# The last matrix product of a two-block layer stack as seven products of half blocks, on one core

## The chip, the cores and the metric

The kernel runs on one core of a Trainium2 chip. The metric is device microseconds of one launch: 3528.63 us, the median of 3 runs (3527.05 to 3533.05). One more execution was taken with the hardware profiler; all rows below come from it.

## The reference, cut to what matters

Two transformer-like blocks run one after the other on 512 tokens of width 2048. The change concerns the last lines of the second block, its feed-forward part and the final norm:

```python
        x = x + y @ w_out[l]
        h = rms_norm(x, norm2_g[l])
        x = x + (jax.nn.silu(h @ ffn_w_gate[l]) * (h @ ffn_w_up[l])) @ ffn_w_down[l]
    return rms_norm(x, final_norm_g)
```

Here `ffn_w_gate` and `ffn_w_up` are 2048 x 5632, `ffn_w_down` is 5632 x 2048, all in float32.

## The kernel before

Every float32 operand is split into two float32r tiles, a high part (`wh` for weights) and a rest (`wl`): `split` (L136, L122) casts on ScalarE (ACT) and subtracts on VectorE (DVE). A product of two operands is then three TensorE matmuls: high x high, low x high and high x low.

`finish` (L1710) runs three stages. The first is the output projection `w_out`, which leaves the residual `x3d` in DRAM. The second, the **gate and up stage**, goes through the hidden width in 11 chunks `c` of 512 columns. It computes both products with seven half-size products for eight (a scheme of Strassen's kind): `fast_group` (L1639) takes weight blocks a11, a12 (gate, upper and lower half of the rows) and a21, a22 (up), builds sums of them on VectorE (`chained`, L1650 on), and works through products 1, 7, 5, 6, 4, 3, 2. A product has four **halves** here (index `u`): one weight tile of 128 x 2 x 512, its split, and 12 matmuls of 512 columns, 8 with `wh` and then 4 with `wl`. Weight tiles come through a pool `fr` of 10 buffers. The split tiles have three buffers in turn (two of `wp2`, one of `fw`), so a split can be written once TensorE is through with the half three places before. The chunk's activation is transposed (`pt`) and stored to `ud` in DRAM.

The third, the **down stage**, is the plain product `ud @ ffn_w_down`: for each of 10 chunks (`down`) and each of 4 column strips, 4 rows of weights times 4 token tiles times 3 matmuls into four `psm` banks, each added to the accumulator `facc` on VectorE. `facc` is loaded from `x3d` first, with `fg`, by 1 MB transfers. The eleventh chunk stands alone as the **last block**: its eight weight tiles are split beforehand, and each token tile is normed and stored right after its matmuls.

Transfers are issued from SP's queue in program order. A scheduler places instructions in each engine's queue by priority and its own estimate; on the chip each queue runs strictly in the order in which it was written.

Of the kernel before, what the change touches and what calls it, by code (L numbers as in the profile page):

```python
# [93 lines left out]
class Kernel:  # L94
# [1508 lines left out]
    def fast_operands(self, pool, za, zb, tiles):  # L1603
        ta, tb = slice(0, 256), slice(256, 512)
        x5 = self.t(pool, [128, 4, 256], F32, "fx5")
        x6 = self.t(pool, [128, 4, 256], F32, "fx6")
        x7 = self.t(pool, [128, 4, 256], F32, "fx7")
# [4 lines left out]
        for i, x in ((1, za[:, :, ta]), (7, x7), (5, x5), (6, x6), (4, None), (3, zb[:, :, tb]), (2, zb[:, :, ta])):  # L1612
            if i == 4:
                x = x7
# [8 lines left out]
    def halves(self, raw, pools):  # L1623
        pools.append(pools.pop(0))
        h = self.t(pools[0], [128, 2, 512], F32R, "wh")
        l = self.t(pools[0], [128, 2, 512], F32R, "wl")
        self.split(h, l, raw)
        return h, l

    def fast_group(self, srcs, X, rp, cp, wps, parts):
# [22 lines left out]
        def part(i, u, opens):  # L1655
            with tc.high_priority(self.ahead):
                h, l = self.halves(weight[i](u), wps)
            at = [(2 * u + kk, kk, t) for kk in range(2) for t in range(2)]

            for j, kk, t in at:  # L1660
                xh, xl = (x[:, j % 4, t * 128:t * 128 + 128] for x in X[j // 4][i])
                self.mm(ps[i][:, t, :], xh, h[:, kk, :], opens and j == 0, False, not opens)
                self.mm(ps[i][:, t, :], xl, h[:, kk, :], False, False, not opens)
            for j, kk, t in at:
                xh = X[j // 4][i][0][:, j % 4, t * 128:t * 128 + 128]
                self.mm(ps[i][:, t, :], xh, l[:, kk, :], False, j == 7, not opens)
# [43 lines left out]
    def finish(self):  # L1710
        tc, nc, a = self.tc, self.nc, self.a
        NC = 11
        ud = self.t(self.dr, [4 * NC, 128, NX], F32, "ud")
        x3d = self.t(self.dr, [4, 128, D], F32, "x3d")
        wg, wu, wd = a["ffn_w_gate_2"][0], a["ffn_w_up_2"][0], a["ffn_w_down_2"][0]
        with self.pool("ff0", 1) as f0:
# [3 lines left out]
            with self.pool("opx", 2) as opx:  # L1720
                X = []
                made = [0]

# [4 lines left out]
                with self.pool("w21", 1) as p1, self.pool("w22", 2) as p2, self.pool("w23", 3) as p3:  # L1728
# [3 lines left out]
                    for n, b in enumerate((0, 2, 1, 3)):  # L1732
# [22 lines left out]
                        else:  # L1755
                            X.append(self.fast_operands(p1, za, z, tiles))
# [10 lines left out]
                with self.pool("fr", 10, side="right") as rp, self.pool("fc", 1) as cp, self.pool("fu", 2) as up, self.pool("fw", 1) as fw:  # L1767
                    wps = [self.wp2, self.wp2, fw]
                    for c in range(NC):
                        cs = slice(c * 512, c * 512 + 512)  # L1770
                        parts = ((0, 1), (2, 3)) if c == 0 else ((0, 1, 2, 3),)
                        for half, (g, u) in zip((1, 0), self.fast_group((wg[:, cs], wu[:, cs]), X, rp, cp, wps, parts)):
                            pt = [self.t(pt_, [128, 512], F32, "pt") for _ in range(2)]
                            for t in range(2):
# [5 lines left out]
                                for f in range(4):  # L1780
                                    o = f % 2 * 256 + t * 128
                                    self.tr(pt[f // 2][:, o:o + 128], s[:, f * 128:f * 128 + 128])
                            for k in range(2):
# [4 lines left out]
            self.raw_pool = self.pool("wq", 3, side="right")  # L1788
            self.wp = self.raw_pool.__enter__()
            self.psum_pools(4, 4)  # L1790
            with self.pool("ff1", 2) as p1, self.pool("ff2", 1) as p2:
                acc = self.t(p2, [128, 4, D], F32, "facc")
                for t in range(4):
                    nc.sync.dma_start(out=acc[:, t, :], in_=x3d[t])
                fg = self.t(p2, [128, D], F32, "fg")
                nc.sync.dma_start(out=fg, in_=a["final_norm_g_2"].rearrange("(o d) -> o d", o=1).to_broadcast([128, D]))

                def hidden(c):
                    u = self.four(F32)
                    nc.sync.dma_start(out=u, in_=ud[c * 4:c * 4 + 4].rearrange("f p t -> p f t"))  # L1800
                    h4, l4 = self.four(F32R), self.four(F32R)
                    self.split(h4, l4, u)
                    return [(h4[:, j, :], l4[:, j, :]) for j in range(4)]

                def down(c, hs):
# [8 lines left out]
                hs = [hidden(0), hidden(1)]  # L1814
                for c in range(NC - 1):
                    down(c, hs[c])
                    if c + 2 < NC:
                        hs.append(hidden(c + 2))

                c = NC - 1  # L1820
                W = []
                for b in range(4):
                    h4, l4 = self.four(F32R), self.four(F32R)
                    for k in range(0, 4, 2):
                        raw = self.t(self.wp, [128, 2, 512], F32, "raw")
# [57 lines left out]
```

## Time and profile before

| | us |
|---|---|
| median of 3 runs | 3528.63 |
| the profiled execution, its time | 3531.79 |
| its span, first to last instruction | 3530.0 |
| gate and up stage, first `un` to the stage change | 2202.5 to about 3026 |
| down stage without the last block | 3025.8 to 3475.7 |
| last block, to the end | 3475.7 to 3530.0 |

The span is what the trace covers; 1.8 us of the execution lie outside it. The profiled execution is 3.2 us above the median of the runs. Matmuls are pipelined: a row's duration is longer than the distance to the next one, so a stretch is costed by the distance.

### The profile page before, as it was taken

The page shows a single profiled execution, that of the slowest core. Times are in us where ns is not written, and L with a number is a line of the kernel's source. Part 1 is how long each engine was busy: PE and PEld are TensorE (multiplying, and loading weights), DVE is VectorE, ACT ScalarE, POOL GpSimd, SP SyncE. Part 2 cuts the span into 40 slices and gives each one's busy share as a digit, 9 for nine tenths or more (in the row PEclk, how much of TensorE's full clock was granted, in tenths as well). Part 3 has the DMA queues.
Part 4 walks back from the last instruction along what each step waited for, and adds up shares of the span by engine and source line. Part 5 has one row for each costly group of instructions (what it writes and reads, how often), then busy time and mean ns, then how long its engine had stood idle before and what let it go on. Part 6 is the DMA issues. An engine that isn't in the chain of part 4 may idle for free.

```text
span 3530.0 us, 48454 instructions
## 1 busy us (share of the span) xinstructions
PE 3438.7 (97%) x18738; PEld 2740.7 (78%) x18738; DVE 2213.8 (63%) x3495; ACT 1367.9 (39%) x2223; POOL 55.1 (2%) x50
## 2 busy tenths in 40 slices
PE   6999999999999999999999998999999999999998
PEld 3488888777778787788777786888888888788887
DVE  4367875466555455764566557778887788555545
ACT  3234444465433323433233334444444444322122
POOL 0000000000000000000000000000000000000000
PEclk8999999999999999999999999999999999999999
DMA  8833433222343443434434543444334335533333
GB/s 283 276 90 89 113 115 109 70 80 63 88 149 124 138 131 97 116 108 132 132 105 144 163 137 108 131 128 123 114 108 125 120 114 160 185 119 119 102 96 108
DMA packets 352602, 442.21 MB, mean 125 GB/s; under 512 B 45871, under 2 KB 200179, under 8 KB 351731
## 3 DMA queue, kind: packets, MB, share of 16 engines
q1 hardware_dynamic: 349456, 437.82, 40.8%
q8 instruction: 147, 2.41, 0.3%
q10 hardware_dynamic: 2915, 1.29, 0.1%
q14 instruction: 84, 0.69, 0.1%
HBM read 383.45 MB, written 55.57 MB: 124 GB/s over the span
## 4 chain that ended last, share of the span: by engine, by line
PE 90%; DMA 5%; DVE 3%; issue 1%; ACT 1%; SPq 0%; POOL 0%; DVEq 0%; POOLq 0%; ACTq 0%
PE acc L112 41%; PE psm L112 23%; PE pp L112 23%; DMA wm<-in_w_mod_dram 2%; PE psm L116 2%; DVE wl L122 1%; PE pt L116 1%; DMA xr<-in_x_dram 0%; DMA raw<-in_ffn_w_down_dram 0%; DVE ga L132 0%; DMA ym<-ysd 0%; DMA fr<-in_ffn_w_gate_dram 0%; DVE op L122 0%; DMA xr<-in_ctx_dram 0%; DMA fr<-in_ffn_w_up_dram 0%
## 5 line engine op out<-in xcount | busy, mean ns | idle before, releaser
L112 PE MATMUL acc<-op,wh 128*128 128x512 f32 (+2 forms) x4160 | 1245.0, 389 | 12.2 <-ACT op L136 4.1
L112 PEld LDWEIGHTS acc<-op,wh 128*128 128x128 f32 (+1 forms) x4160 | 765.1, 190 | 198.8 <-issue 32.2
L122 DVE TENSOR_TENSOR wl<-raw,wh 128x512 fp32r<-128x512 f32 (+4 forms) x464 | 420.8, 907 | 631.6 <-ACT wh L136 597.9
L112 PE MATMUL acc<-op,wl 128*128 128x512 f32 (+2 forms) x2080 | 768.3, 389 | 4.9 <-DVE wl L122 4.7
L136 ACT CAST wh<-raw 128x512 fp32r<-128x512 f32 (+4 forms) x464 | 369.1, 796 | 991.4 <-PE acc L112 597.5
L112 PE MATMUL pp<-wh,op 128*128 128x512 f32 x2112 | 529.7, 393 | 10.1 <-ACT wh L136 10.1
L136 ACT CAST wh<-fr 128x1024 fp32r<-128x1024 f32 x308 | 322.9, 1052 | 400.8 <-PE pp L112 352.8
L112 PEld LDWEIGHTS pp<-wh,op 128*128 128x128 f32 x2112 | 397.5, 188 | 98.8 <-ACT wh L136 10.2
L112 PEld LDWEIGHTS acc<-op,wl 128*128 128x128 f32 (+1 forms) x2080 | 389.7, 189 | 98.9 <-issue 18.5
L122 DVE TENSOR_TENSOR wl<-fr,wh 128x1024 fp32r<-128x1024 f32 x308 | 371.0, 1219 | 103.8 <-ACT wh L136 67.0
L112 PE MATMUL psm<-wh,op 128*128 128x512 f32 x1280 | 396.6, 391 | 7.3 <-DVE facc L122 7.3
L112 PEld LDWEIGHTS psm<-wh,op 128*128 128x128 f32 x1280 | 241.6, 189 | 58.2 <-issue 7.7
L112 PE MATMUL pp<-wl,op 128*128 128x512 f32 x1056 | 285.4, 392 | 0.1
L112 PE MATMUL psm<-wl,op 128*128 128x512 f32 x640 | 250.2, 391 | 0.3 <-DVE wl L122 0.3
L122 DVE TENSOR_TENSOR fr<-fr,fr 128x1024 f32<-128x1024 f32 x176 | 210.9, 1220 | 47.4 <-DMA fr<-in_ffn_w_gate_dram 28.8
L112 PEld LDWEIGHTS pp<-wl,op 128*128 128x128 f32 x1056 | 197.7, 188 | 43.8 <-DVE wl L122 0.8
L122 DVE TENSOR_TENSOR facc<-facc,psm 128x512 f32<-128x512 f32 x176 | 117.9, 685 | 60.1 <-PE psm L112 54.3
L112 PEld LDWEIGHTS psm<-wl,op 128*128 128x128 f32 x640 | 120.8, 189 | 25.6 <-DVE wl L122 0.7
L112 PE MATMUL acc<-wh,op 128*128 128x256 f32 x576 | 113.6, 292 | 0.0
L112 PEld LDWEIGHTS acc<-wh,op 128*128 128x128 f32 x576 | 90.9, 191 | 5.0 <-issue 3.6
L112 PE MATMUL pp<-wh,opx 128*128 128x512 f32 x352 | 93.8, 399 | 0.0
L112 PE MATMUL acc<-wl,op 128*128 128x256 f32 x288 | 84.4, 294 | 1.0 <-DVE wl L122 0.9
(474 smaller groups left out, 3521.3 us busy)
## 6 DMA issues: line engine op xcount, KB each, us to landing
raw<-in_w_in_dram SPq DMA_DIRECT2D x216, 256.0 KB, 2.8
fr<-in_ffn_w_gate_dram SPq DMA_DIRECT2D x88, 512.0 KB, 4.2
fr<-in_ffn_w_up_dram SPq DMA_DIRECT2D x88, 512.0 KB, 4.2
raw<-in_ffn_w_down_dram SPq DMA_DIRECT2D x88, 512.0 KB, 4.0
wm<-in_w_mod_dram SPq DMA_DIRECT2D x64, 512.0 KB, 5.5
raw<-in_w_out_dram SPq DMA_DIRECT2D x64, 512.0 KB, 3.8
raw<-in_w_in_dram SPq DMA_DIRECT2D x240, 128.0 KB, 2.3
wm<-in_w_mod_dram SPq DMA_DIRECT2D x64, 256.0 KB, 2.9
```

The lines of the kernel that those rows point to most:

```text
L112: self.nc.tensor.matmul(out, lhsT=l, rhs=r, start=start, stop=stop, skip_group_check=more)
L116: self.nc.tensor.transpose(out, x, self.ident[0:n, 0:n])
L122: (e or self.nc.vector).tensor_tensor(out=out, in0=x, in1=y, op=op)
L136: self.nc.scalar.copy(h, x)
```

## The change

The down stage now uses seven products for eight as well, over pairs of chunks. `X` is the hidden state of two chunks, cut by tokens (first and last 256) and by rows of the hidden width; the weights of two chunks are cut into a11, a12, a21, a22 for each 1024 columns (`v` = 0, 1).

- The token operands 5, 6, 7 and 4 are sums of the transposed activation. They are made in the gate and up stage by four VectorE instructions in each of 10 chunks, and seven tiles instead of four go to `ud`.
- In the down stage, each pair of chunks loads seven operand tiles and splits them. For each `v` the products run in the order 1, 7, 2, 5, 4, 6, 3, with two halves each. Only product 5's weight sum (a21 + a22) is made on VectorE (`both`). The sums for 7, 6 and 3 are made in place in a11's tile by accumulating transfers that GpSimd's queue (POOL) issues (`plus`): a11 + a21, then + a22, then + a12. Product 7 follows product 1, and 3 follows 6, on the same tile.
- PSUM stays with the gate and up stage's three `pp` double banks; products 2, 4 and 3 are accumulated on top of 1, 7 and 5. `facc` is first written by products, and `x3d` is added to it by eight accumulating transfers.
- The pool `fr` of 10 buffers is kept through the down stage, and the last block's weights and `fg` are loaded through it early.

Core of the diff:

```diff
-                                v = self.t(up, [128, 2, 256], F32, "v")
-                                nc.scalar.copy(v, pt[k].rearrange("p (f t) -> p f t", f=2))
-                                f = c * 4 + k * 2
-                                nc.sync.dma_start(out=ud[f:f + 2, :, half * 256:half * 256 + 256].rearrange("f p t -> p f t"), in_=v)
+                                nc.scalar.copy(vs[k], pt[k].rearrange("p (f t) -> p f t", f=2))
+                            if half:
+                                b12, b22 = vs
+                                continue
+                            b11, b21 = vs
+                            out = [(1, b11), (2, b21), (3, b22)]
+                            if c < NC - 1:
+                                x5, x6 = (self.t(up, [128, 512], F32, "s").rearrange("p (f t) -> p f t", f=2) for _ in range(2))
+                                self.tt(x5, b11, b12, ALU.subtract)
+                                self.tt(b12, b12, b22, ALU.subtract)
+                                self.stt(x6, b22, -1.0, x5, ALU.mult, ALU.subtract)
+                                out += [(5, x5), (7, b12), (6, x6)]
...
+                            for i, x in out:
+                                nc.sync.dma_start(out=ud[i - 1, c].rearrange("f p t -> p f t"), in_=x)
+                            if c < NC - 1:
+                                self.tt(b21, b21, x6, ALU.add)
+                                nc.sync.dma_start(out=ud[3, c].rearrange("f p t -> p f t"), in_=b21)
...
-                for t in range(4):
-                    nc.sync.dma_start(out=acc[:, t, :], in_=x3d[t])
...
-                    for b in range(4):
-                        ps = [self.psm() for _ in range(4)]
-                        self.block(wd[c * 512:c * 512 + 512], [(b * 512, 512)], 4,
-                                   [(ps[t], "t", (t, 0), hs, True, True) for t in range(4)])
-                        for t in range(4):
-                            v = acc[:, t, b * 512:b * 512 + 512]
-                            self.tt(v, v, ps[t], ALU.add)
...
+                order = (1, 7, 2, 5, 4, 6, 3)
+
+                def operands(c):
+                    X = {}
+                    with tc.high_priority(400):
+                        for i in order:
+                            x = raw().rearrange("p a (b t) -> p (a b) t", t=256)
+                            nc.sync.dma_start(out=x, in_=ud[i - 1, 2 * c:2 * c + 2].rearrange("g f p t -> p (g f) t"))
+                            o = self.four(F32R)
+                            h, l = (o[:, k:k + 2, :].rearrange("p a (b t) -> p (a b) t", t=256) for k in (0, 2))
+                            self.split(h, l, x)
+                            X[i] = (h, l)
+                    return [X]
...
+                    def plus(name, u):
+                        nc.gpsimd.dma_start(out=W["a11", u], in_=load(name, u), accum_op=ALU.add)
+                        return W["a11", u]
+
+                    def both(u):
+                        x, y = plain("a21", u), plain("a22", u)
+                        self.tt(x, x, y, ALU.add)
+                        return x
+
+                    weight = {
+                        1: lambda u: plain("a11", u), 7: lambda u: plus("a21", u), 2: lambda u: plain("a12", u),
+                        5: both, 4: lambda u: W["a22", u], 6: lambda u: plus("a22", u), 3: lambda u: plus("a12", u),
+                    }
...
+                    onto = {2: 1, 4: 7, 3: 5}
+                    to = {1: U, 7: A22, 2: A11, 5: A22, 4: A21, 6: U, 3: A12}
+                    for i in order:
+                        ps[i] = ps[onto[i]] if i in onto else bank()
+                        for u in range(2):
+                            with tc.high_priority(self.ahead):
+                                h, l = self.halves(weight[i](u), wps)
+                            self.product(X, i, ps[i], h, l, 2 * u, i not in onto, 3)
+                        if c == 0 and i not in (5, 6):
+                            nc.scalar.copy(to[i], ps[i])
+                        else:
+                            self.tt(to[i], to[i], ps[i], ALU.subtract if i == 5 else ALU.add)
+                    if c == 0:
+                        for t in range(4):
+                            o = slice(v * 1024, v * 1024 + 1024)
+                            nc.gpsimd.dma_start(out=acc[:, t, o], in_=x3d[t][:, o], accum_op=ALU.add)
```

`product` holds the 12 matmuls that `part` in `fast_group` had, in the same order; `order` gives the seven products their numbers.

How the instructions stand. First TensorE's queue at the change of stage. Before, the transposes (`pt`) of the last activation stand among the down stage's first matmuls (`psm`):

```order
L112 MATMUL psm_4435_25726<-wh_4442_25761,op_4430_25716 128x512
L112 MATMUL psm_4436_25727<-wh_4442_25761,op_4429_25715 128x512
L116 MATMUL pt_4420_25660<-ident_11_107,s_4422_25662 128x128 x2
L116 MATMUL pt_4421_25661<-ident_11_107,s_4422_25662 128x128 x2
L116 MATMUL pt_4420_25660<-ident_11_107,s_4423_25670 128x128 x2
L116 MATMUL pt_4421_25661<-ident_11_107,s_4423_25670 128x128 x2
L112 MATMUL psm_4436_25727<-wl_4443_25762,op_4429_25715 128x512
L112 MATMUL psm_4436_25727<-wh_4442_25761,op_4430_25716 128x512
L112 MATMUL psm_4437_25728<-wh_4442_25761,op_4429_25715 128x512
L112 MATMUL psm_4437_25728<-wl_4443_25762,op_4429_25715 128x512
L112 MATMUL psm_4437_25728<-wh_4442_25761,op_4430_25716 128x512
```

Now, behind product 1's first half (`pp_4463` with `wh_4465`) and the transposes of `s_4427`, comes product 7 (`pp_4470`), then the next transposes, and only then product 1's second half (`wh_4468`):

```order
L116 MATMUL pt_4425_25663<-ident_11_107,s_4428_25673 128x128 x2
L116 MATMUL pt_4426_25664<-ident_11_107,s_4428_25673 128x128 x2
L112 MATMUL pp_4470_25864<-wh_4471_25866,op_4452_25798 128x512 x8
L112 MATMUL pp_4470_25864<-wl_4472_25867,op_4452_25798 128x512 x4
L116 MATMUL pt_4440_25751<-ident_11_107,s_4442_25753 128x128 x2
L116 MATMUL pt_4441_25752<-ident_11_107,s_4442_25753 128x128 x2
L116 MATMUL pt_4440_25751<-ident_11_107,s_4443_25761 128x128 x2
L116 MATMUL pt_4441_25752<-ident_11_107,s_4443_25761 128x128 x2
L112 MATMUL pp_4463_25826<-wh_4468_25847,op_4450_25793 128x512 x8
L112 MATMUL pp_4463_25826<-wl_4469_25848,op_4450_25793 128x512 x4
L112 MATMUL pp_4470_25864<-wh_4473_25883,op_4452_25798 128x512 x8
L112 MATMUL pp_4470_25864<-wl_4474_25884,op_4452_25798 128x512 x4
```

The two halves of products 1 and 7 have moved into each other, with the transposes between them. In the nine later pairs of `c` and `v` the products stand one after the other.

Second VectorE in the middle of the down stage. Before, two splits (`wl`) and four additions to `facc` alternate:

```order
L122 TENSOR_TENSOR wl_4592_26732<-raw_4590_26729,wh_4591_26731 128x1024
L122 TENSOR_TENSOR wl_4599_26770<-raw_4597_26767,wh_4598_26769 128x1024
L122 TENSOR_TENSOR facc_4426_25706<-facc_4426_25706,psm_4583_26695 128x512
L122 TENSOR_TENSOR facc_4426_25706<-facc_4426_25706,psm_4584_26696 128x512
L122 TENSOR_TENSOR facc_4426_25706<-facc_4426_25706,psm_4585_26697 128x512
L122 TENSOR_TENSOR facc_4426_25706<-facc_4426_25706,psm_4586_26698 128x512
L122 TENSOR_TENSOR wl_4602_26800<-raw_4600_26797,wh_4601_26799 128x1024
L122 TENSOR_TENSOR wl_4612_26844<-raw_4610_26841,wh_4611_26843 128x1024
```

Now, at the change from one `v` to the next: product 3's splits (`wl_4634`, `wl_4636`), product 6's sum to `au1`, product 1's splits on the new tiles `fr_4652` and `fr_4655`, product 3's addition to `facc`, and then product 7's splits on the same two tiles:

```order
L122 TENSOR_TENSOR wl_4634_26872<-fr_4598_26647,wh_4633_26871 128x1024
L122 TENSOR_TENSOR wl_4636_26889<-fr_4601_26665,wh_4635_26888 128x1024
L122 TENSOR_TENSOR au1_4448_25790<-au1_4448_25790,pp_4628_26834 128x1024
L122 TENSOR_TENSOR wl_4654_26944<-fr_4652_26941,wh_4653_26943 128x1024
L122 TENSOR_TENSOR wl_4657_26962<-fr_4655_26959,wh_4656_26961 128x1024
L122 TENSOR_TENSOR facc_4446_25788<-facc_4446_25788,pp_4615_26757 128x2x512
L122 TENSOR_TENSOR wl_4660_26981<-fr_4652_26941,wh_4659_26980 128x1024
L122 TENSOR_TENSOR wl_4662_26998<-fr_4655_26959,wh_4661_26997 128x1024
L122 TENSOR_TENSOR au0_4447_25789<-au0_4447_25789,pp_4651_26940 128x1024
```

Between a tile's first split (`wl_4654`) and its second (`wl_4660`) the accumulating transfer into `fr_4652` has to take place; two VectorE instructions stand between.

POOL's queue, which issued no transfer before, now has six for each pair of `c` and `v`, two each for products 7, 6 and 3; each waits for the split that reads the tile before it.

## Rows read from the trace of the kernel before

**Rows 1.** The page, parts 1 and 4: busy time by engine; chain by engine.

```profile
PE 3438.7 (97%) x18738; PEld 2740.7 (78%) x18738; DVE 2213.8 (63%) x3495; ACT 1367.9 (39%) x2223; POOL 55.1 (2%) x50
...
PE 90%; DMA 5%; DVE 3%; issue 1%; ACT 1%; SPq 0%; POOL 0%; DVEq 0%; POOLq 0%; ACTq 0%
```

**Rows 2.** Windows: busy us and instructions of each engine, clock, DMA share, GB/s.

```profile
0.00:40.00 40.00, 20.30 (x101) 16.26 (x102) 20.71 (x42) 20.82 (x53) 1.53 (x5) 0.83 0.91 282
...
2205.00:3020.00 815.00, 814.94 (x3629) 667.01 (x3628) 659.48 (x601) 375.46 (x396) 0.00 (x0) 1.00 0.41 125
3060.00:3440.00 380.00, 380.00 (x1677) 314.76 (x1678) 190.91 (x216) 81.79 (x74) 0.00 (x0) 1.00 0.37 112
```

**Rows 3.** Chain of work, down stage: start, duration, what, instructions.

```profile
3039.20 4.93 DMA facc<-x3d
...
3059.85 391.31 PE psm L112 x1725
```

**Rows 4.** PE in order of time, around the stage change: idle before in brackets.

```profile
3025.82 0.39 PE L112 MATMUL psm<-wh,op 128*128 128x512 f32 x1
...
3032.87 1.04 PE L116 MATMUL pt<-ident,s 128*128 128x128 f32 x8
...
3045.15 0.77 PE L112 MATMUL psm<-wh,op 128*128 128x512 f32 x1 [7.34 <-DVE facc L122]
```

**Rows 5.** PE in order of time, before the last block.

```profile
3475.73 8.46 PE L112 MATMUL psm<-op,op 128*128 128x512 f32 x29 [2.83 <-DVE facc L122]
```

**Rows 6.** Windows of PE after the two gaps: busy, granted clock, DMA.

```profile
3045.00:3051.00 6.00, 5.85 (x15) 0.54 1.02 431
...
3475.70:3478.00 2.30, 2.27 (x8) 0.82 0.65 198
3478.00:3480.00 2.00, 2.00 (x6) 0.50 0.22 83
```

**Rows 7.** PE in order of time: two shorter gaps earlier in the program.

```profile
259.34 0.50 PE L112 MATMUL acc<-op,wl 128*128 128x512 f32 x1 [1.24 <-DVE wl L122]
...
1872.34 0.78 PE L112 MATMUL acc<-op,wh 128*128 128x512 f32 x2 [1.85 <-DVE st L122]
```

**Rows 8.** Windows of PE behind those two gaps.

```profile
259.30:261.00 1.70, 1.66 (x7) 1.00 0.64 207
...
1872.30:1874.00 1.70, 1.66 (x5) 0.68 0.51 166
1874.00:1876.00 2.00, 2.00 (x6) 0.50 0.25 35
```

**Rows 9.** Groups of the gate and up stage: busy us, mean ns of one, idle before.

```profile
L122 DVE TENSOR_TENSOR wl<-fr,wh 128x1024 fp32r<-128x1024 f32 x277 | 333.5, 1219 | 88.9 <-ACT wh L136 56.4 <-PE pp L112 31.9
L136 ACT CAST wh<-fr 128x1024 fp32r<-128x1024 f32 x276 | 289.2, 1052 | 355.1 <-PE pp L112 316.7 <-DVE fr L122 13.9 <-issue 9.9
...
L1785 ACT COPY v<-pt 128x512 f32<-128x512 f32 x38 | 20.4, 587 | 19.5 <-PE pt L116 19.5
...
L132 DVE SCALAR_TENSOR_TENSOR s<-s,un 128x512 f32<-128x512 f32 x20 | 12.8, 683 | 0.0
L122 DVE TENSOR_TENSOR un<-pp,un 128x1024 f32<-128x1024 f32 x10 | 12.2, 1223 | 12.7 <-PE pp L112 12.7
```

**Rows 10.** The page, part 6: transfers, KB each, median us from issue to landing.

```profile
raw<-in_ffn_w_down_dram SPq DMA_DIRECT2D x88, 512.0 KB, 4.0
wm<-in_w_mod_dram SPq DMA_DIRECT2D x64, 512.0 KB, 5.5
...
ud<-v SPq DMA_DIRECT2D x44, 256.0 KB, 2.2
op<-ud SPq DMA_DIRECT2D x11, 1024.0 KB, 6.9
...
facc<-x3d SPq DMA_DIRECT2D x4, 1024.0 KB, 9.0
```

**Rows 11.** DVE in order of time: three splits back to back.

```profile
2579.27 3.49 DVE L122 TENSOR_TENSOR wl<-fr,wh 128x1024 fp32r<-128x1024 f32 x3
```

More of the change, by code (lines that the diff above doesn't have):

```diff
@@ L1628, in halves, with product @@
         return h, l
+    def product(self, X, i, ps, h, l, j0, opens, last):
+        at = [(j0 + kk, kk, t) for kk in range(2) for t in range(2)]
+        for j, kk, t in at:
+            xh, xl = (x[:, j % 4, t * 128:t * 128 + 128] for x in X[j // 4][i])
+            self.mm(ps[:, t, :], xh, h[:, kk, :], opens and j == 0, False, not opens)
+            self.mm(ps[:, t, :], xl, h[:, kk, :], False, False, not opens)
+        for j, kk, t in at:
+            xh = X[j // 4][i][0][:, j % 4, t * 128:t * 128 + 128]
+            self.mm(ps[:, t, :], xh, l[:, kk, :], False, j == last, not opens)
     def fast_group(self, srcs, X, rp, cp, wps, parts):
@@ L1657, in part @@
                 h, l = self.halves(weight[i](u), wps)
[L1658 to L1666, printed above, removed]
+            self.product(X, i, ps[i], h, l, 2 * u, opens, 7)
         def bank():
@@ L1722, in finish @@
                 made = [0]
+                fx = iter(range(100))
                 def tiles():
@@ L1755, in finish @@
                         else:
-                            X.append(self.fast_operands(p1, za, z, tiles))
+                            X.append(self.fast_operands(lambda: self.t(p1, [128, 4, 256], F32, f"fx{next(fx) % 3}"), za, z, tiles))
                     r = self.token_rsq(f0, s3, D, 1e-6, "r3s")
@@ L1815, in finish @@
[L1815 to L1821, printed above, removed]
-                for b in range(4):
-                    h4, l4 = self.four(F32R), self.four(F32R)
-                    for k in range(0, 4, 2):
-                        raw = self.t(self.wp, [128, 2, 512], F32, "raw")
-                        nc.sync.dma_start(out=raw, in_=wd[c * 512 + k * 128:c * 512 + k * 128 + 256, b * 512:b * 512 + 512].rearrange("(k p) c -> p k c", p=128))
-                        self.split(h4[:, k:k + 2, :], l4[:, k:k + 2, :], raw)
-                    W.append((h4, l4))
+                au = [self.t(p2, [128, 2, 512], F32, f"au{v}") for v in range(2)]
@@ new lines, in finish @@
+                X = operands(0)
+                for c in range(NC // 2):
+                    down(c, 0, X)
+                    down(c, 1, X)
+                    if c + 1 < NC // 2:
+                        X = operands(c + 1)
+                c = NC - 1
+                with tc.high_priority(400):
+                    u = self.four(F32)
+                    for i, f, o in ((1, 0, 0), (5, 0, 256), (2, 2, 0), (3, 2, 256)):
+                        nc.sync.dma_start(out=u[:, f:f + 2, o:o + 256], in_=ud[i - 1, c].rearrange("f p t -> p f t"))
+                    uh, ul = self.four(F32R), self.four(F32R)
+                    self.split(uh, ul, u)
+                    W = []
+                    for b in range(4):
+                        h4, l4 = self.four(F32R), self.four(F32R)
+                        for k in range(0, 4, 2):
+                            r = raw()
+                            nc.sync.dma_start(out=r, in_=wd[c * 512 + k * 128:c * 512 + k * 128 + 256, b * 512:b * 512 + 512].rearrange("(k p) c -> p k c", p=128))
+                            self.split(h4[:, k:k + 2, :], l4[:, k:k + 2, :], r)
+                        W.append((h4, l4))
+                    fg = []
+                    for i in range(2):
+                        fg.append(raw())
+                        nc.sync.dma_start(out=fg[i].rearrange("p a b -> p (a b)"),
+                                          in_=a["final_norm_g_2"][i * 1024:i * 1024 + 1024].rearrange("(o d) -> o d", o=1).to_broadcast([128, 1024]))
```

70 lines of the change are left out of this document (42 added, 28 removed).

## The prediction

> **What bounds the kernel now.** I read the page first: PE is busy 97% of the span, and the chain of work lies on PE for 90% [rows 1]. The windows by stage then show that this share is no average over unlike stages here: from 2205 to 3020 PE works 814.94 of 815 us and from 3060 to 3440 all of 380, at a granted clock of 1.00, while VectorE is busy 659.48 us (81%) and 190.91 us (50%) [rows 2]. So both stages that the change touches end when TensorE ends, and a matmul that is left out is time saved, as long as nothing starts to make TensorE wait. The chain gives the price of one: 391.31 us for 1725 matmuls [rows 3], 0.2268 us each, so a half (12 matmuls) is 2.72 us. Around the down stage PE has two gaps: 7.34 us for the `facc` load and 2.83 us before the last block [rows 3 to 5]. After each the granted clock falls: 0.54 over the 6 us after the first, 0.50 in a stretch after the second [rows 6]; 0.5 is the 1.2 GHz level. In the first, 15 matmuls took 6 us where 3.4 would do, a loss of 2.4 us; in the second it is about 1.3. A gap of 1.85 us still brings such a fall, one of 1.24 us does not [rows 7, 8].
>
> **What it removes.** Before, the down stage has 10 x 4 x 4 x 4 x 3 = 1920 matmuls without the last block; after, 5 pairs x 2 `v` x 7 products x 2 halves x 12 = 1680. That is 240 x 0.2268 = **54.4 us** less. From 3025.82 to 3475.73 the stage took 449.9 us [rows 4, 5]; with the slow clock behind its second gap, 451.2.
>
> **The change of stage.** The load of `facc` that caused the 7.34 us gap is gone, but the new order puts product 7's first half and the transposes between product 1's halves, and this is a chain. Take the end of the last gate and up matmul as 0. The split for product 1's first half can end at about -3.1 (its place in the three split buffers comes free at -5.4; one sum and it follow, 1.22 us each [rows 9]). Then the accumulating transfer goes, for a time L. With L = 6.9 (below) it lands at 3.8, the cast adds 1.05 [rows 9], and PE, which is there at 3.5 (2.72 and eight transposes, some 0.8), waits 1.4 us. Product 1's second half uses the third split buffer, now in a new pool over tiles of the stage before, and its cast waits for two of the last `ud` stores: after the transposes two copies of 0.59, a store of 2.2 and the cast of 1.05 [rows 9, 10], 4.5 to 5 us of gap. Product 7's second half needs a transfer that can start only when that tile's split is done, 1.22 us after the cast, when PE still has 1.5 us of the half to run; then L and a cast: 6.9 + 1.05 - 1.5, 6.4 us of gap. Sum 12.5, and two falls of the clock at 1.6 to 2.4: **16.5 us** where it was 9.8. With L = 4.0 it is about 12, with L = 9.0 about 21.
>
> **The links.** In the other nine pairs of `c` and `v`, product 7 follows 1 and 3 follows 6 on the same tile, and with product 3 of the first pair these are 19 links. What they cost hangs on L. The tile's first split waits until the split buffer three halves back is free, 5.44 us before its product starts; VectorE does one addition from PSUM (1.22) and the split (1.22) [rows 9], so the transfer starts 3.0 us ahead of the product. The next product's cast must end 5.44 us after that start and takes 1.05. So L may be 3.0 + 5.44 - 1.05, less 0.2 for signals: **7.2 us**. Queued behind a late transfer are ACT's cast, VectorE's split and, since these queues are in order, every later split and addition; PE waits for them.
>
> L has no row: no accumulating transfer runs before. From below it is a plain load of the same 512 KB, 4.0 us, or 5.5 in the busiest stretch [rows 10], at a DMA share of about 0.9 [rows 2]. From above it is `facc<-x3d`, 1024 KB, 9.0 us, four at once [rows 10]. The addition has to read its destination too, so twice the bytes move; nearest is `op<-ud`, 1024 KB in an otherwise ordinary stretch, 6.9 us [rows 10]. I take that: 0.3 us inside the margin. Transfers scatter, so I allow 19 x 0.25 = **5 us**. At 9.0 each link is 1.8 us late and the clock falls as well (1.6): 3.4 x 19 = 65 us. At 4.0: nothing.
>
> Here a page of the Trainium skill would be more generous. "DMA: Bandwidth & Descriptors", section "Anatomy of one DMA", fits 2.0 us plus bytes over 436 GB/s to a transfer of GpSimd's queue, an estimate of 3.2 us for 512 KB without an addition; by it all links are hidden and the sum is 5 us and part of the change of stage better. The plain row, 4.0 us, is slower than that, so I stay with the row.
>
> **The rest.** *VectorE in the gate and up stage* gets four more instructions for each of 10 chunks, 0.68 us each [rows 9], 2.7 in 79 (28 halves and 32 transposes): 81% becomes 84%, hidden under PE; without cover 27 us. The stores stand ahead of two weight loads in SP's queue that are used about two halves (5.4 us) later; such a load takes 4.0 us [rows 10], so nothing. *VectorE in the down stage*: per pair of `c` and `v` 14 splits, 2 sums, 7 additions, and for `v` = 1 seven operand splits too: 30 instructions. Back to back three take 3.49 us [rows 11], so 35 of 38.1 us (14 halves), and 27 for `v` = 0: it fits, with little to spare; at 1.22 each it would be 36.6. *DMA*: each 76 us carries 23 plain and 12 accumulating 512 KB pieces, 18.4 MB or 241 GB/s, with the second reading 324, against 112 now; the rows show 282 at a share of 0.91 over 40 us and 431 for a short time [rows 2, 6]. Enough, but transfers will meet. *End*: the last block's weights are there early, so the 2.83 us gap shrinks to about 1; the last token tile's additions stand behind the norm of the one before, +1.
>
> **Sum** for the profiled execution: after, 381.0 + 1.6 (transposes, now all behind the stage's start) + 16.5 + 5 + 1 + 1 = 406 in place of 451.2, so -45 on 3531.8: 3487. That execution lies 3.2 us over the median of the runs, so the forecast in their terms is 3528.6 - 45 = **3483 us**.
>
> **The rivals.** Differences under 0.2% (7 us) a measurement of this kernel can hardly tell from no change.
>
> *Late links (slower).* Under load the accumulating transfer takes 9.0 us or more. Then TensorE stops 19 times for over 1.8 us and works at 1.2 GHz after each: 65 us and 4 more at the change of stage, less the 50 saved otherwise: 3548; each further us of L adds 19. It decides from L of just under 9, where the clock starts to fall. For it speaks the 9.0 row, against it that that row is four transfers of 1 MB.
>
> *VectorE holds the issue.* If POOL could get a transfer out only while VectorE pauses, up to 3.49 us of back-to-back work [rows 11] come on top of 4.0 to 5.5: L = 7.5 to 9.0, 6 to 34 us, 3485 to 3515. The Trainium skill, "SBUF — State Buffer", "SBUF: two separate sides", says that VectorE in its two-port modes keeps GpSimd from writing descriptors; under "Who interferes with whom" it says that `tensor_tensor` has no such mode. No row shows either, since POOL issues nothing before. Nearly all of VectorE's work here is `tensor_tensor`, so I give it little.
>
> *The DMA engines become the bound.* At 282 GB/s for a share of 0.91, a full share is 310, and 324 asked takes 381 x 324 / 310 = 398: +17, 3500. Against it speaks 431 GB/s.
>
> *VectorE becomes the bound* with 30 instructions at 1.22 and its waits: a few us in each `v` = 1, some 10 in all, 3493.
>
> **Chances.** Forecast, L up to 8 (3473 to 3498): 0.50. VectorE's hold 0.09, DMA 0.10, VectorE 0.05; late links with L of 9 and more 0.20; about even (L near 8.8) 0.06. Faster holds the forecast and all but a little of the next three, 0.72; same 0.06; slower 0.22. The range is 3468 (L = 4.0 and no slow clock at the change of stage) to 3546, which cuts off the worse half of the late links. The forecast's own range is 3473 to 3498.
>
> **What would show it.** Matmul records 240 fewer at 0.227 us; a PE gap of 12 us in all near 3026 to 3045, with 0.5 clock behind it; `fr<-in_ffn_w_down` on POOL landing in about 7 us; PE's waits for the cast `wh` nearly empty in mid-stage; no new PE wait before 3020. It is wrong if the landings are 9 us and PE stops before products 7 and 3 of each pair, or if VectorE idles less than 2% there.

## The result and the profile after

The changed kernel takes 3570.86 us, the median of 4 runs (3563.4 to 3576.01), beside 3530.84 us for the kernel before (4 runs): a ratio of 1.011, with a 95% interval of 1.0098 to 1.0123. It is 40 us slower, where 45 us faster was forecast, and outside the range. The page, parts 1 and 4, answers to [rows 1]:

```profile
PE 3420.4 (96%) x18498; PEld 2712.5 (76%) x18498; DVE 2316.8 (65%) x3546; ACT 1451.2 (41%) x2318; POOL 134.4 (4%) x118
...
PE 76%; DMA 9%; issue 8%; DVE 4%; ACT 1%; POOL 1%; SPq 0%; POOLq 0%; DVEq 0%; ACTq 0%
```

The 240 matmuls are gone (18738 to 18498), but the chain lies on PE for 76% instead of 90%. The windows, beside [rows 2], say where. Columns are PE, PEld, DVE, ACT and POOL busy, then granted clock, DMA share, GB/s:

```profile
2205.00:3020.00 815.00, 815.00 (x3632) 667.74 (x3631) 679.42 (x641) 373.00 (x396) 0.00 (x0) 1.00 0.44 134
3020.00:3060.00 40.00, 28.68 (x108) 22.36 (x107) 18.72 (x20) 14.56 (x18) 4.98 (x4) 0.83 0.65 165
3060.00:3440.00 380.00, 333.47 (x1339) 263.30 (x1338) 238.07 (x204) 149.56 (x149) 65.12 (x56) 0.93 0.83 204
```

The gate and up stage is untouched: PE works all of 815 us. In the down stage PE pauses, and the clock is at 0.93. From 3020 to 3530 PE waits 27 times, 68.8 us in all (each line: what it waited for, us in total, times, longest):

```profile
PE pp L112 <- ACT wh L136: 57.4, 24, 4.4
PE pp L112 <- ACT au L1875: 10.6, 1, 10.6
PE pp L112 <- DVE wl L122: 0.8, 2, 0.4
```

Three of the gaps are the change of stage, against the one of 7.34 us in [rows 4] (PE in order of time):

```profile
3026.66 1.99 PE L112 MATMUL pp<-wh,op 128*128 128x512 f32 x8
...
3034.10 2.78 PE L112 MATMUL pp<-wh,op 128*128 128x512 f32 x8 [3.67 <-ACT wh L136]
...
3043.94 3.78 PE L112 MATMUL pp<-wh,op 128*128 128x512 f32 x8 [4.35 <-ACT wh L136]
...
3052.57 3.58 PE L112 MATMUL pp<-wh,op 128*128 128x512 f32 x8 [3.30 <-ACT wh L136]
```

They make 11.3 us. Of the other 24 gaps, about 19 stand ahead of product 7 or product 3, whose accumulating transfer goes onto the tile of the product just before. Eight matmuls that take 2.0 us elsewhere take up to 3.78 after a gap, at a granted clock of 0.50. Waits (68.8) and clock (an estimate from the shares: 7% of 380 us and 17% of 40, some 33) are 102 us; before they were 9.8 at the change of stage and about 4 ahead of the last block. The 88 us more swallow the 54.4 saved and leave 34 of the 40 us lost. Most of the remaining 6 lies at the gaps as well: a single matmul's row is 0.39 us where the distance to the next one is 0.23, so each of the 24 additional gaps costs some 0.16 more, about 4 us by this estimate. The DMA queues and landings of 3040 to 3530, beside [rows 10]:

```profile
q0 software_dynamic: 17076, 34.88, 42.4%
q1 hardware_dynamic: 37920, 58.20, 35.2%
...
fr<-in_ffn_w_down_dram SPq DMA_DIRECT2D x78, 512.0 KB, 5.2
fr<-in_ffn_w_down_dram POOLq DMA_DIRECT2D x58, 512.0 KB, 7.1
fr<-ud SPq DMA_DIRECT2D x28, 512.0 KB, 7.0
facc<-x3d POOLq DMA_DIRECT2D x8, 512.0 KB, 10.6
```

The accumulating transfer takes 7.1 us from issue to landing (the prediction's L); 6.9 was assumed. So L was right, and the margin that it had to fit was not. One link shows it, 6 to 3 in the pair `c` = 2, `v` = 0. Chosen rows from the time line of four engines, sorted by start:

```profile
3257.08 1.05 ACT L136 CAST wh<-fr 128x1024 fp32r<-128x1024 f32 x1 [1.72 <-PE pp L112]
3259.80 1.05 ACT L136 CAST wh<-fr 128x1024 fp32r<-128x1024 f32 x1 [1.67 <-PE pp L112]
3261.54 1.23 DVE L122 TENSOR_TENSOR fr<-fr,fr 128x1024 f32<-128x1024 f32 x1 [3.94 <-DMA fr<-in_ffn_w_down_dram]
3262.68 1.22 DVE L122 TENSOR_TENSOR wl<-fr,wh 128x1024 fp32r<-128x1024 f32 x1
3263.82 1.22 DVE L122 TENSOR_TENSOR facc<-facc,pp 128x1024 f32<-128x1024 f32 x1
3264.95 1.22 DVE L122 TENSOR_TENSOR wl<-fr,wh 128x1024 fp32r<-128x1024 f32 x1
3266.04 1.98 PE L112 MATMUL pp<-wh,op 128*128 128x512 f32 x8
3266.47 1.20 POOL L1853 DMA_DIRECT2D fr<-in_ffn_w_down_dram  x1 [17.27 <-DVE wl L122]
3272.54 1.04 ACT L136 CAST wh<-fr 128x1024 fp32r<-128x1024 f32 x1 [8.92 <-DMA fr<-in_ffn_w_down_dram]
3273.64 2.87 PE L112 MATMUL pp<-wh,op 128*128 128x512 f32 x7 [1.91 <-ACT wh L136]
```

ACT casts product 6's first half at 3259.80, 6.2 us ahead of its matmuls (3266.04), as early as the split buffer allows. The subtraction for it, `wl`, stands on VectorE behind the sum `fr<-fr,fr` for product 5 of the *next* pair, which waits 3.94 us for its loads. It runs at 3264.95 and ends at 3266.17, not 3.0 us ahead of the product but 0.1 behind its start. The transfer starts 0.3 us later and takes 6 us; product 3 waits 1.91 us.

The other links agree. Take the first half of each from the first pair's product 3 to product 3 of `c` = 4, `v` = 0, and compare POOL's start with the first matmul of the product that reads the tile before. The median lead is 0.0 us ahead of product 7 (1.2 ahead to 1.1 behind) and 0.0 ahead of product 3 (2.7 ahead to 2.7 behind), where the forecast had 3.0. These transfers landed after a median of 6.8 and 6.0 us, so with the forecast's lead most of them would have been in time.

### The profile page after: what moved, and what is told of

It reads as the page before. It is cut to its first block, busy times and chain, and to the rows that moved or that the text cites. A ratio compares the mean times of both kernels' runs of the same rounds, so it can differ in the third digit from the quotient of the medians.

```text
span 3571.9 us, 48466 instructions
## 1 busy us (share of the span) xinstructions
PE 3420.4 (96%) x18498; PEld 2712.5 (76%) x18498; DVE 2316.8 (65%) x3546; ACT 1451.2 (41%) x2318; POOL 134.4 (4%) x118
## 4 chain that ended last, share of the span: by engine, by line
PE 76%; DMA 9%; issue 8%; DVE 4%; ACT 1%; POOL 1%; SPq 0%; POOLq 0%; DVEq 0%; ACTq 0%
PE acc L112 40%; PE pp L112 24%; PE psm L112 10%; DMA fr<-in_ffn_w_down_dram 4%; DMA wm<-in_w_mod_dram 2%; PE psm L116 2%; DVE wl L122 1%; DMA fr<-ud 1%; PE pt L116 0%; POOL fr L1853 0%; DVE op L122 0%; DVE ga L132 0%; DMA ym<-ysd 0%; DMA fr<-in_ffn_w_gate_dram 0%; ACT wh L136 0%
## 5 line engine op out<-in xcount | busy, mean ns | idle before, releaser
L112 PE MATMUL pp<-wh,op 128*128 128x512 f32 x3232 | 832.8, 401 | 78.0 <-ACT wh L136 67.5
L112 PEld LDWEIGHTS pp<-wh,op 128*128 128x128 f32 x3232 | 618.6, 192 | 228.8 <-ACT wh L136 80.1
L136 ACT CAST wh<-fr 128x1024 fp32r<-128x1024 f32 x448 | 466.5, 1050 | 641.8 <-PE pp L112 424.5
L122 DVE TENSOR_TENSOR wl<-fr,wh 128x1024 fp32r<-128x1024 f32 x448 | 541.1, 1221 | 202.1 <-ACT wh L136 170.3
L122 DVE TENSOR_TENSOR wl<-raw,wh 128x512 fp32r<-128x512 f32 (+4 forms) x384 | 323.0, 841 | 460.0 <-ACT wh L136 422.8
L136 ACT CAST wh<-raw 128x512 fp32r<-128x512 f32 (+4 forms) x384 | 284.8, 742 | 678.9 <-PE acc L112 588.5
L112 PE MATMUL pp<-wl,op 128*128 128x512 f32 x1616 | 443.3, 397 | 0.8 <-DVE wl L122 0.8
L112 PEld LDWEIGHTS pp<-wl,op 128*128 128x128 f32 x1616 | 308.5, 192 | 70.8 <-DVE wl L122 2.4
L122 DVE TENSOR_TENSOR fr<-fr,fr 128x1024 f32<-128x1024 f32 x196 | 235.5, 1220 | 76.0 <-DMA fr<-in_ffn_w_down_dram 32.4
L1853 POOL DMA_DIRECT2D fr<-in_ffn_w_down_dram x60 | 72.6, 1219 | 1271.8 <-DMA fr<-in_ffn_w_down_dram 906.9
L112 PEld LDWEIGHTS pp<-wh,opx 128*128 128x128 f32 x352 | 65.4, 188 | 14.0
```

The lines of the kernel that those rows point to most:

```text
L112: self.nc.tensor.matmul(out, lhsT=l, rhs=r, start=start, stop=stop, skip_group_check=more)
L122: (e or self.nc.vector).tensor_tensor(out=out, in0=x, in1=y, op=op)
L136: self.nc.scalar.copy(h, x)
L1853: nc.gpsimd.dma_start(out=W["a11", u], in_=load(name, u), accum_op=ALU.add)
```

## The experiments

First the links themselves. *Overwriting instead of adding*:

```diff
-nc.gpsimd.dma_start(out=W["a11", u], in_=load(name, u), accum_op=ALU.add)
+nc.gpsimd.dma_start(out=W["a11", u], in_=load(name, u))
```

> The 60 transfers of GpSimd's queue overwrite their tile instead of adding to it (the three weight sums of products 7, 6 and 3 are left out); queue, place, bytes and the dependence on the split of the product before stay. Theory A (lost lead: the transfer starts when the product before starts instead of 3.0 us ahead of it, and 7 us then do not fit into the 5.44 us of a product): without the second access the landing falls from 7.1 to about 5.3 us, each link is 1.8 us less late but not in time, so about half of the gaps stay: 3520 to 3540. Theory B (the DMA engines' load delays every transfer, the plain ones too): the share in the down stage falls from 0.79 to about 0.57, plain weight loads fall from 5.2 to 4.2 us and nearly all gaps go: 3485 to 3500. Theory C (the operand casts of the next pair, scheduled ahead on ACT and VectorE, hold the weights' casts back whatever the transfers do): 3555 or more.

3523.92 us (ratio 0.9976, 0.9966 to 0.9986). The landing on POOL's queue falls to 4.9 us (3040 to 3530), and PE's gaps to 38.0 us in 19 (3020 to 3530):

```profile
fr<-in_ffn_w_down_dram SPq DMA_DIRECT2D x78, 512.0 KB, 5.1
fr<-in_ffn_w_down_dram POOLq DMA_DIRECT2D x58, 512.0 KB, 4.9
```

```profile
PE pp L112 <- ACT wh L136: 26.1, 15, 4.1
PE pp L112 <- ACT au L1875: 8.5, 1, 8.5
PE pp L112 <- DVE wl L122: 3.4, 3, 1.7
```

*A tile of its own*:

```diff
-nc.gpsimd.dma_start(out=W["a11", u], in_=load(name, u), accum_op=ALU.add)
-return W["a11", u]
+x = raw()
+nc.gpsimd.dma_start(out=x, in_=load(name, u))
+return x
```

> The 60 transfers of GpSimd's queue load a tile of their own, plainly (the same three sums are left out): as the overwriting run in bytes and queue, but none waits for the split of the product before. Theory A: all links are gone, what stays are the change of stage and the 10.6 us wait behind the operand casts: 3571 less 50 us of gaps and 25 of slow clock, 3490 to 3505, and clearly below the overwriting run. Theory B: the same time as the overwriting run, within 5 us. Theory C: 3555 or more.

3483.02 us (0.9861, 0.9845 to 0.9878), five gaps of 8.7 us in all ahead of matmuls and one of 0.2 ahead of a transpose. The waits of PE from 3020 to 3530:

```profile
PE pp L112 <- DVE wl L122: 5.9, 1, 5.9
PE pp L112 <- ACT wh L136: 2.8, 4, 1.1
PE pt L116 <- DVE s L132: 0.2, 1, 0.2
```

So 88 us come back without the links: 47 with the addition, 41 more with the dependence, though the landing is no shorter in the second (5.2 us) than in the first (4.9). The split is good to a few us only, since with each edit the scheduler orders the queues anew (at the change of stage the transposes stand elsewhere in the second run). Theory B needed the two alike. With L = 4.9 links are still late: ahead of product 7 the transfer starts at a median of 0.3 us behind the start of product 1, so the margin there is under 5 us and not 7.2. Operands and pair sum were still there in the run with tiles of its own, in the same bunch, and cost little: they matter through the links.

*Spaced order*, the whole computation:

```diff
-order = (1, 7, 2, 5, 4, 6, 3)
+order = (1, 5, 2, 7, 6, 4, 3)
...
-7: lambda u: plus("a21", u)  6: lambda u: plus("a22", u)  3: lambda u: plus("a12", u)
+7: lambda u: plus("a11", "a21", u)  6: lambda u: plus("a21", "a11", u)  3: lambda u: plus("a21", "a12", u)
```

(the first argument is the tile added to; product 5's tile holds a21 + a22; not shown: products 7 and 5 take their PSUM banks together, and for `c` = 0 product 5 is written to `facc` negated by ScalarE, since it now comes first)

> The whole computation with the products in the order 1, 5, 2, 7, 6, 4, 3: product 7's weights are summed onto product 1's tile two products later, product 6's onto product 5's tile two products later, product 3's onto product 6's one product later, so each accumulating transfer has 5.4 to 10.9 us more, with the same number of transfers, bytes and VectorE instructions. Theory A: the gaps at the links go, 3490 to 3515, with the landing of the accumulating transfers still at 7 us or more and the DMA share near 0.8. Theory B: the load is the same, so the time stays at 3560 to 3575. Theory C: the same, 3560 or more.

3525.48 us (0.9986, 0.9976 to 0.9995): 45 us less at the same bytes and a share of 0.89, so B falls, but 10 us more than A gave. What stayed in mid-stage is for the larger part (14 of 25 us) one gap of 2.3 to 4.6 us ahead of product 7 in the `v` = 1 pair of each of the first four `c`, where ACT stands on operand casts. A group of ACT from 3060 to 3440:

```profile
L136 ACT CAST op<-fr 128x1024 fp32r<-128x1024 f32 x32 | 33.6, 1049 | 68.4 <-DMA fr<-ud 59.3 <-DMA fr<-in_ffn_w_down_dram 9.1
```

*Sums on VectorE*, the whole computation:

```diff
-nc.gpsimd.dma_start(out=W["a11", u], in_=load(name, u), accum_op=ALU.add)
+x = raw()
+nc.sync.dma_start(out=x, in_=load(name, u))
+self.tt(W["a11", u], W["a11", u], x, ALU.add)
```

> The three sums as plain loads into tiles of their own by SP's queue and additions on VectorE, the whole computation. VectorE gets 6 more instructions of 1.22 us in each pair of c and v: 36 in a pair with operand splits, about 43 us in 38.1, and 29, 34 us, in the others. Theory A: the links are gone but VectorE is the bound in every second pair, 5 us each and what it holds back at the next: 3515 to 3540. Theory B: the DMA load is that of the overwriting run, so VectorE alone counts: 3510 to 3530. Theory C: the operand splits lengthen VectorE's queue too: 3560 or more.

3503.67 us (0.992, 0.9906 to 0.9935), better than each theory gave, and faster than both kernels. VectorE works 89% of mid-stage, and PE is busy for 362.61 of 380 us, against 333.47 in the changed kernel:

```profile
3060.00:3440.00 380.00, 362.61 (x1540) 288.40 (x1538) 337.79 (x294) 173.82 (x171) 7.25 (x8) 0.99 0.73 233
```

Next, what took the lead away. *No pair sum*: `self.tt(x, x, y, ALU.add)` left out of `both`.

> VectorE's sum of a21 and a22 for product 5 is left out, both loads stay; the accumulating transfers stay as they are. Theory A (the lead of the first split is lost in the in-order queues: the pair sum stands on VectorE ahead of the splits of products 4 and 6 and waits there for its two loads, the operand casts of the next pair stand on ACT ahead of the weights' casts; with a lead of 3.0 us a landing of 7 us is hidden): the gaps ahead of product 3 in the pairs with v = 0 and those ahead of product 7 that follow from them go, those of the pairs with v = 1 stay: 3530 to 3548. Theory B (the accumulating transfer under load is too long whatever the lead is): the sum was one of 30 VectorE instructions, 3560 to 3570.

*No later operands*: `X = operands(c + 1)` left out.

> The products of all pairs use the token operands of c = 0: the 28 later loads, their casts and splits are left out, and the transfers, links and sums on weights stay. Theory A: the gaps of the pairs with v = 1 go (among them the 10.6 us behind the operand casts), those ahead of product 3 in the pairs with v = 0 stay, and VectorE has room to make up for them: 3520 to 3540. Theory B: a tenth less DMA load and nothing else at the links, 3555 to 3565 without the 10.6 us.

*Neither*:

> Both are left out, the pair sum and the later operands; all 60 accumulating transfers stay on their tiles and in their links. Theory A: first splits end 3 us ahead of their product in mid-stage again, the landings stay near 6.5 to 7 us and nearly all links are hidden; what stays is the change of stage, some 16 us, and a few stretched transfers: 3490 to 3505. Theory B: most links stay late, 3525 or more.

3546.82, 3547.34 and 3514.4 us: 24.0, 23.5 and 56.5 us less than the changed kernel. The first is as theory A had it, the second 7 us worse, the third lies between the theories. Why is plain in its time line. Chosen rows from the pair `c` = 1, `v` = 1:

```profile
3187.14 1.05 ACT L136 CAST wh<-fr 128x1024 fp32r<-128x1024 f32 x1 [1.72 <-PE pp L112]
3189.21 1.22 DVE L122 TENSOR_TENSOR wl<-fr,wh 128x1024 fp32r<-128x1024 f32 x1
3190.74 1.20 POOL L1853 DMA_DIRECT2D fr<-in_ffn_w_down_dram  x1 [14.17 <-DVE wl L122]
3193.34 2.03 PE L112 MATMUL pp<-wh,op 128*128 128x512 f32 x8
3196.78 1.05 ACT L136 CAST wh<-fr 128x1024 fp32r<-128x1024 f32 x1 [5.82 <-DMA fr<-in_ffn_w_down_dram]
3198.88 1.98 PE L112 MATMUL pp<-wh,op 128*128 128x512 f32 x8
3199.29 2.95 ACT L136 CAST wh<-fr 128x1024 fp32r<-128x1024 f32 x3 [1.45 <-DMA fr<-in_ffn_w_down_dram]
3202.64 2.36 DVE L122 TENSOR_TENSOR wl<-fr,wh 128x1024 fp32r<-128x1024 f32 x2
3204.16 2.44 POOL L1853 DMA_DIRECT2D fr<-in_ffn_w_down_dram  x2 [10.44 <-DVE wl L122]
3204.40 2.00 PE L112 MATMUL pp<-wh,op 128*128 128x512 f32 x8
3210.30 1.04 ACT L136 CAST wh<-fr 128x1024 fp32r<-128x1024 f32 x1 [8.06 <-DMA fr<-in_ffn_w_down_dram]
3211.40 2.13 PE L112 MATMUL pp<-wh,op 128*128 128x512 f32 x8 [1.38 <-ACT wh L136]
```

Product 6's split (the second row) ends at 3190.43, 2.9 us ahead of its matmuls at 3193.34: the lead of the forecast. Its transfer and the signals around it take 6.35 us, and product 3 starts at 3198.88 without a wait. But ACT cast product 3's halves only as their tiles landed, at 3196.78 and 3199.29, and the casts for the next product 1 are queued behind the second of them, two of the three in that row. So product 1's split ends only 0.5 us ahead of its matmuls (3204.40), and product 7, after much the same time, is 1.38 us late. From the second pair to the last, each has such a gap ahead of product 7, 1.2 to 2.9 us. The first halves of the other links before the last pair show the same two cases: ahead of product 3 the transfer starts 2.6 to 2.7 us before product 6 each time, and PE never waits; ahead of product 7 it starts between 0.2 us before product 1 and 0.7 us behind its start, and PE waits each time. With the pair sum alone left out the lead of 2.6 to 2.7 us ahead of product 3 is back in all pairs with `v` = 0, without a wait; in three of the first four with `v` = 1 it is 1.2 to 1.3 us, and product 3 waits 1.6 to 3.4 us.

Three tries at a better order. *Spaced, spread, and product 3's sum on VectorE*:

```diff
+self.tt(W["a12", u], W["a12", u], W["a21", u], ALU.add)
...
-3: lambda u: plus("a21", "a12", u)
+3: lambda u: W["a12", u]
...
+n = order.index(i) + 7 * v
+if c + 1 < NC // 2 and n in at:
+    Y[order[at.index(n)]] = operand(c + 1, order[at.index(n)])
...
-X = operands(c + 1)
+X = [Y]
```

(the sum stands behind product 6's split; `operand` loads and splits one operand; `at` is 0, 2, 4, 5, 6, 8, 10)

> The whole computation with three edits: the spaced order 1, 5, 2, 7, 6, 4, 3; the next pair's token operands loaded and split one by one over the two pairs, after products 1, 2, 6, 4 and 3 of v = 0 and after 5 and 7 of v = 1, not all seven in a bunch; product 3's weights made on VectorE from the a12 tile that product 2 has left, so that 20 of the 60 accumulating transfers fall away. Theory (two causes, each seen alone: links that follow each other and lose their lead, and operand casts that stand on ACT for their loads): both go, the DMA share falls under 0.75, VectorE carries about 27 to 30 instructions in every pair; 3485 to 3500. Rival (VectorE in order is the bound once it works over 85 per cent, or ten raw tiles are too few to load ahead): 3505 to 3525.

*The same without the VectorE sum*:

> The spaced order of 3525.5 us with the operands spread as in the run beside it; all 60 accumulating transfers stay. Theory: the operand waits on ACT were most of what stayed in the spaced order, one of 3 to 4.6 us in each c and the slow clock behind it: 3498 to 3512. Rival (the DMA share of 0.89 stretches all transfers): 3518 to 3526.

*The same without the spread*:

> The spaced order with product 3's weights made on VectorE, operands in a bunch as before: 20 accumulating transfers fewer, two VectorE instructions more in each pair. Theory: the bunched operand casts stay, but their loads land earlier at a lower DMA share: 3510 to 3522. Rival (the DMA share was the cause in the spaced order): 3495 to 3505.

3527.88 (0.9989, 0.9979 to 0.9999), 3517.32 (0.9957, 0.9943 to 0.997) and 3539.7 us (1.0023, 1.0012 to 1.0034). Spreading the operands gives 8 to 12 us, less than expected; the sum on VectorE costs 10 to 14 although the DMA share falls from 0.91 to 0.77. All three theories miss; the middle run comes within 1 us of its rival's range. In the two runs with the sum VectorE waits 46 and 62 us for the weight loads of its sums (3060 to 3440), against 28 and 36 in the two without it. That keeping a12's tile until product 3 leaves too few of the ten raw tiles was not tried.

*The spread alone in the changed kernel*:

> The changed kernel with one edit: the next pair's operands loaded and split one by one over the two pairs; products 1, 7, 2, 5, 4, 6, 3, all 60 accumulating transfers and the pair sum stay. Theory A (the bunch of operand casts is worth what leaving the operands out was worth, 23 us, the rest being the pair sum's wait and the two links that follow each other): 3543 to 3556. Theory B (what leaving the operands out saved was the smaller load on the DMA engines and on VectorE): 3563 to 3571.

3557.26 us (1.0067, 1.0054 to 1.0079): 13.6 us less than the changed kernel, where leaving the operands out gave 23.5. So somewhat over half of that goes with the place of the operand casts; that the rest is their load is not shown. The time lies just over A's bound and under B's.

*Sums on VectorE with the spread*, and *product 6's sum given back to a transfer*:

> The whole computation: the three sums as plain loads and additions on VectorE (3503.7 us with bunched operands) and the next pair's operands loaded and split one by one over the two pairs. Theory (in that run TensorE waited in the pairs with v = 1, where VectorE had 36 instructions and ACT stood on operand loads): the work is spread to some 34 and 31 instructions in a pair and the waits for operand loads go: 3485 to 3496. Rival (VectorE at 89 per cent is the bound whatever the spread): 3500 to 3508.

> The version of 3503.4 us (sums on VectorE, operands spread, the order 1, 7, 2, 5, 4, 6, 3) with one sum given back to a transfer: product 6's, which adds a22 onto product 7's tile three products after its split, so that the transfer has some 19 us. VectorE has two instructions fewer in each pair. Theory (an accumulating transfer costs nothing where it has products between, and VectorE at 88 per cent is what stays): 3490 to 3500. Rival (the second access of the transfers stretches the plain loads and what VectorE gains is lost there): 3501 to 3512.

3503.35 us (0.9914, 0.99 to 0.9927) and 3508.28 us (0.9934, 0.992 to 0.9947). Both theories miss and both rivals hold: without links the spread gives nothing, and giving product 6's sum to a transfer with three products of room gains nothing either (5 us more).

Last, *operand subtractions on GpSimd* in the version with sums on VectorE:

```diff
-self.split(h, l, x)
+nc.scalar.copy(h, x)
+self.tt(l, x, h.bitcast(F32), ALU.subtract, nc.gpsimd)
```

> The whole computation: the three sums as plain loads and additions on VectorE as in the run before of that kind (3503.7 us), and the subtraction of the operand splits on GpSimd, where 128 x 512 took 1.09 us, so that 128 x 1024 should take 2.2 us: 35 times 1.22 us less on VectorE. Theory A: with no accumulating links only VectorE's load in the pairs with v = 1 was left, and it goes: 3485 to 3495. Rival: GpSimd's subtraction slows VectorE down or comes too late for the products, 3500 to 3515.

3529.96 us (0.999, 0.9981 to 0.9999), 26 us worse: the rival's side, and 15 us beyond its range. VectorE was not relieved: it worked 334.98 of the 380 us of mid-stage, against 337.79. More on it at the end.

## Why the prediction was wrong, step by step

*What is removed* was right: 240 matmuls fewer, and the run whose transfers go to tiles of their own lands at 3483 us, 48 us under before. That this is the forecast's number is chance: it has no late links, but it also lacks most of the change of stage that the forecast held.

*The change of stage* was right as a sum: gaps of 3.67, 4.35 and 3.30 us against 1.4, 4.5 to 5 and 6.4 and, with the clock at 0.83 over 40 us (6.8 us), 18 in place of 16.5. Product 7's first half waited 2.3 us longer than forecast and its second half 3.1 less, so that the sum came out is in part luck.

*The links* are the step that failed: "The tile's first split waits until the split buffer three halves back is free", and from that a lead of 3.0 us and a margin of 7.2. Two things were taken for granted there. The first is that nothing else stands ahead of the split: VectorE's order put the next pair's sum before it, and in the pairs with `v` = 1 ACT's order put operand casts before it, each waiting for loads of 5 to 7 us. The measured lead was 0.0 us at the median in place of 3.0; taking both out brings it back ahead of product 6 (2.9 us from the split's end), and 56.5 us with it. The second is that each of the 19 links may use its margin for itself: product 7 follows four halves behind product 3, and a landing that uses up the first lead leaves 0.5 us for the second. The sentence that says so ("Queued behind a late transfer are ACT's cast, VectorE's split and, since these queues are in order, every later split and addition") was applied to transfers that are late, not to one that is just in time. The term of 5 us measured about 70: 88 for all links, less some 17 (10 of gaps, 7 of clock) at the change of stage, which the run with tiles of its own hardly has. Some 13 of the 70, also absent from that run, are the longest gap below (10.6, and 2.8 of slow matmuls behind it).

That gap, 10.58 us, stands at no link. ACT, in order, stood on two operand casts ahead of the copy that has to read product 1's PSUM before product 2 is added to it:

```profile
3102.84 1.04 ACT L136 CAST op<-fr 128x1024 fp32r<-128x1024 f32 x1 [4.97 <-DMA fr<-ud]
3103.79 1.04 ACT L136 CAST wh<-fr 128x1024 fp32r<-128x1024 f32 x1
3109.51 1.04 ACT L136 CAST op<-fr 128x1024 fp32r<-128x1024 f32 x1 [4.68 <-DMA fr<-ud]
3110.46 1.00 ACT L1875 COPY au<-pp 128x1024 f32<-128x1024 f32 x1
```

*VectorE in the gate and up stage* was right: 679.42 of 815 us (83%), hidden. *The second access* was right in kind: per MB the accumulating queue took twice the engines' time of the plain one (42.4% for 34.88 MB, 35.2% for 58.20). What it costs the other transfers the runs do not settle. Plain weight loads went from 4.0 to 5.2 us, but took 5.1 in the run that only overwrites, so most of that is there without the addition too; in the spaced order they took 6.0.

*The rivals.* "Late links" had the right side and place and about the right price (65 us), but the wrong condition: it wanted L of 9, and 7.1 was enough because the lead was gone. "VectorE holds the issue" did not come: in the time line of the run with neither, POOL issues at 3204.16 while VectorE works from 3202.64 to 3205.00. The DMA engines did not become the bound: the spaced and spread version has a share of 0.91 and is 54 us faster than the changed kernel at 0.83. VectorE was no bound at 63%; at 89%, in the fastest complete version, it may be one, which no run shows by itself.

For L itself, the estimate of 3.2 us from the Trainium skill, "DMA: Bandwidth & Descriptors", section "Anatomy of one DMA", is not borne out here: a plain transfer of 512 KB on GpSimd's queue took 4.9 to 5.2 us among the others, an accumulating one 7.1. The measurement decides.

## What to carry to other kernels

A margin worked out from when buffers come free holds only if nothing else stands in the in-order queues between. So list what is queued ahead of the instruction that starts the transfer, and what each of those waits for. Count chained links together, since one that lands just in time has used the lead of the next. A sum in place by transfer is cheap in instructions and dear in latency (7.1 us here, against 4.9 for the plain transfer). Give it a tile that nobody has to finish reading first, or let VectorE add while it has room: that made this change pay, 3503.67 us against 3530.8.

## What the runs showed of the hardware

GpSimd's subtraction of 128 x 1024 took 3.1 us, not the 2.2 scaled from 128 x 512, and it slowed some of VectorE's operations, not all. Groups of the run with the subtractions on GpSimd, 3060 to 3440, mean ns behind the comma:

```profile
L122 DVE TENSOR_TENSOR wl<-fr,wh 128x1024 fp32r<-128x1024 f32 x120 | 176.2, 1478 | 16.1 <-ACT wh L136 11.1 <-PE pp L112 4.6
L122 DVE TENSOR_TENSOR fr<-fr,fr 128x1024 f32<-128x1024 f32 x71 | 102.1, 1453 | 17.6 <-DMA fr<-in_ffn_w_down_dram 16.9
L122 DVE TENSOR_TENSOR facc<-facc,pp 128x1024 f32<-128x1024 f32 x37 | 44.9, 1213 | 11.3 <-PE pp L112 11.1
...
L122 POOL TENSOR_TENSOR op<-fr,op 128x1024 fp32r<-128x1024 f32 x28 | 86.7, 3132 | 202.7 <-ACT op L1832 141.5 <-PE pp L112 61.2
```

VectorE's operations with both inputs in SBUF went from 1220 ns, in the version with all subtractions on VectorE, to over 1450 on average; the one with an input in PSUM took 1213, against 1215 there. The Trainium skill, "SBUF — State Buffer", "Who interferes with whom", says that VectorE with two SBUF inputs shares a read port with GpSimd's reads; these rows agree.

An accumulating transfer also costs more to issue: POOL's instruction took 1.22 us on average for the 60 in the changed kernel, 0.73 for the 60 that overwrote.
